# Four hidden tiles of the `down` projection by half products, in pieces between the `up` tiles

## The chip, the core and the metric

The kernel runs on one core of a Trainium2 chip. The metric is device time in microseconds (us), from the start of one execution to its end. A core has TensorE (PE; its weight loads are listed as PEld), VectorE (DVE), ScalarE (ACT), GpSimd (POOL), which here mostly issues DMAs, and SyncE (SP), which issues the other DMAs. TensorE writes into PSUM, whose tiles are allocated as banks of 128 partitions by 512 float32 values; VectorE and ScalarE read results from there. Each engine works through its own list of instructions in order and waits by semaphores for the others.

## The reference

One decoder layer on 512 positions of width 1024: a mixer (pooling and sparse attention), then a gated MLP with a short convolution. The change is in the MLP:

```python
h = rms_norm(x, ffn_norm_g[l])
gate_pre, val = jnp.split(h @ w_up[l], 2, axis=-1)      # D_FF = 2816
gate_c = causal_dwconv(gate_pre, conv_w[l], conv_b[l])  # width 3
x = x + (jax.nn.silu(gate_c) * val) @ w_down[l]
```

The hidden width of 2816 is 22 tiles of 128, called `f` below; the output width of 1024 is 8 tiles.

## The kernel before

**Precision.** Every float32 operand `v` is split into a part `hi` (type fp32r) and the rest `lo = v - hi`; a product is the sum of three matmuls: hi by hi, hi by lo, lo by hi. `split` (line 462) does it with one ScalarE copy and one VectorE subtraction. `split_by_dma` (line 1269) does it with two ScalarE passes and an accumulating DMA issued by POOL, and without VectorE.

**The order.** The code does not issue instructions where it names them. `Plan` (line 117) notes each one with its reads and writes, prices it (`price`), tries several orders in a model of the engines and DMA queues (`run`, `dues`, `emit`) and in the end writes out the best order, engine by engine interleaved in time (lines 429 to 431; for this reason all instructions have line 431 in the profile). In the MLP TensorE's own order is that of the code; the other engines are ordered by the time at which TensorE needs their results. In PSUM the planner tracks a whole tile at a time, unless its name is in the set `fine`, in which case it tracks columns (line 190); nothing in this kernel adds a name to it. Semaphores between engines are made afterwards, from the order that was written out.

**Memory.** Most data lies in 60 pages of 128 x 512 values (`page`). A page named by `soon` is for weights prepared ahead; these are given out in the order of the code and only while more than `AHEAD` = 4 pages are free. Weights land in rings of three buffers, `wraw`, `whi`, `wlo`, 1024 values wide (`ring`).

**Half products.** A product of a 2 x 2 block matrix of weights with a 2 x 2 block matrix of data (two groups of tiles by two halves of 256 positions) is done with seven block products instead of eight. It needs sums of weight blocks, made by VectorE (`half_weights`, line 1410), and sums of the data (`y_sums`, line 1338). `product` (line 1147) issues one block product: for each tile three matmuls of 256 columns. The partial sums stay in three banks `bx`, `by`, `bq`; where a second result continues from a first, ScalarE copies `bx` into `by` and TensorE goes on adding there.

**The loop.** For `f` from 0 to 21 (line 1487) the kernel computes the gate and value tiles (`up_plain` for tile 0, `up_fast`, line 1441, for the others, by seven half products of four tiles each), the convolution and SiLU (`conv`), and splits the result `y` (`split_y`, line 1349). The last two products of a tile, `end1` and `end2`, are held back (`held`) and issued inside the next tile.

**`down` before.** The 22 hidden tiles are taken in groups: `GROUPS` has tiles 0 to 4, 5 to 9 and 10 to 13, and tiles 14 to 21 (from `LAST`) are left for the end. `dn_group` (line 1398) makes, for one group, eight pieces, one for each output tile: load 128 x (640 or 512) weights, split them, 15 or 12 matmuls of 512 columns into bank `sc`, and add the result to `x2[f]` on VectorE. The pieces go into the list `fills`. At `f` = 6, 12 and 16 (`AT`) a group is put into the list, and the four numbers of `FILL[f]` say how many pieces are taken out before the tile and at three places within `up_fast`: `n1` after the first `bq` product or the held product in its place, `n3` after the first `by` product and the second held one, `n2` after the second `bx` product. What is left goes behind the last tile. Then `dz_fast` (line 1508) does tiles 14 to 21 by half products, four pairs of output tiles, and stores the results.

Of the kernel before, what the change touches and what calls it, by code (L numbers as in the profile page):

```python
# [9 lines left out]
F32R = mybir.dt.float32r  # L10
I32 = mybir.dt.int32
AF = mybir.ActivationFunctionType
# [3 lines left out]
P = 128  # L16
T = 512
# [6 lines left out]
FF = 2816  # L24
KF = 22
LAST = 14
GROUPS = ((0, 5), (5, 10), (10, 14))
EPS = 1e-6
BIG = 1e30

# [24 lines left out]
PLAIN = (0,)  # L55
DIRECT = (0,)
FASTM = (0, 1)
AT = (6, 12, 16)
FILL = {f: (0, 0, 0, 0) for f in range(22)}
FILL.update({f: (0, 1, 1, 0) for f in (7, 10, 13, 16,)})  # L60
FILL.update({f: (0, 1, 0, 0) for f in (6, 8, 9, 11, 12, 14, 15, 17, 18, 19,)})
TRIES = 12
RESERVE = 3
CUTS = (1, 2)
# [4 lines left out]
SHARE = 1.5  # L69
LANDS = (0.8, 0.8, 1.2, 1.2, 2.0, 2.0)  # L70
TRIALS = ((0.5, RATE), (0.8, RATE), (1.4, RATE), (0.8, 0.9 * RATE))
AHEAD = 4
RUN = 12


# [357 lines left out]

@with_exitstack
def hybrid_layer(ctx: ExitStack, tc: tile.TileContext, xT, xa, pos, par, cst, poolw, w1, wa, wb, wf,
                 wpo, wno, wout, wup, wdn, wdz, out):
    nc = tc.nc
    pl = Plan(nc)
    PE, ACT, DVE, POOL, SP = pl.engines
# [8 lines left out]
    def page(name, shape=(P, T), dt=F32):  # L448
        return pl.tile(sb, shape, dt, name, "pg", PAGES)
# [12 lines left out]
    def split(dst_hi, dst_lo, src, scale=None):  # L462
        if scale is None:
            ACT.activation(dst_hi, src, AF.Copy)
            DVE.tensor_sub(dst_lo, src, f32(dst_hi))
        else:
            ACT.activation(dst_hi, src, AF.Copy, scale=scale)
            DVE.scalar_tensor_tensor(dst_lo, src, scale, f32(dst_hi), op0=ALU.mult, op1=ALU.subtract)
# [40 lines left out]
    H2 = T // 2  # L509
# [18 lines left out]
    w2 = R("w2").rearrange("p (a b) -> p a b", a=2)  # L528
# [109 lines left out]
    A, KQ, KH, KL = (ang[:, i] for i in range(4))  # L638
# [47 lines left out]
    for c, (k0, k1) in enumerate(((0, 3), (3, 6), (6, 8))):  # L686
        raw = ring("wraw")
        SP.dma_start(raw[:, :(k1 - k0) * 280], flat(wb[:, k0:k1]))
        for j in range(k1 - k0):
            home = ("pp", 10) if len(bw) < 5 else ("pt", 6)  # L690
            hi, lo = (pl.tile(sb, (P, 280), F32R, n, home[0], home[1]) for n in ("bh", "bl"))
# [42 lines left out]
    for t in range(NT):  # L734
        x, y = qp[t], kp[t]
# [182 lines left out]
    x = keep("kcx", (64, 1, DH))  # L918
# [248 lines left out]
    for c in range(4):  # L1167
        if c not in FASTM:
# [3 lines left out]
            for a in range(2):  # L1172
                f, o = 2 * c + a, a * 512
# [19 lines left out]
        rg, hi, lo = ring("wraw"), ring("whi", F32R), ring("wlo", F32R)  # L1193
        SP.dma_start(rg, flat(wno[c]))
        split(hi[:, :T], lo[:, :T], rg[:, :T])
        a11, a12, a21, a22 = (rg[:, q * H2:(q + 1) * H2] for q in range(4))
        s3, e3, hi2, lo2 = soon("s3")[:, :H2], soon("sh", F32R), soon("sh", F32R), soon("sl", F32R)
# [7 lines left out]
        w11, w12, w2, w4 = ((hi[:, q * H2:(q + 1) * H2], lo[:, q * H2:(q + 1) * H2]) for q in range(4))  # L1205
        w1, w5 = ((hi2[:, q], lo2[:, q]) for q in (L, Rr))
        w3 = e3[:, L], e3[:, Rr]
        bx, bq, by = any_bank(), any_bank(), any_bank()
# [6 lines left out]
        half = page("u1")  # L1215
# [117 lines left out]
        ACT.activation(t, t, AF.Silu)  # L1333
        return t

    yth, ytl, ylast = {}, {}, {}

    def y_sums(k):
        b1, b2 = ylast[k], ylast[k + 4]
        ta, tb = page("ta"), page("tb")  # L1340
        DVE.tensor_sub(ta[:, :H2], b1[:, :H2], b1[:, H2:])
        DVE.tensor_sub(tb[:, :H2], b2[:, H2:], b1[:, H2:])
        DVE.scalar_tensor_tensor(ta[:, H2:], ta[:, :H2], -1.0, b2[:, H2:], op0=ALU.mult, op1=ALU.subtract)
        DVE.scalar_tensor_tensor(tb[:, H2:], ta[:, H2:], -1.0, b2[:, :H2], op0=ALU.mult, op1=ALU.subtract)
        for i, x in ((0, ta), (1, tb)):
            yth[k - LAST, i], ytl[k - LAST, i] = page("yth", dt=F32R), page("ytl", dt=F32R)
            split(yth[k - LAST, i], ytl[k - LAST, i], x)

    def split_y(f, y):
        yh[f], yl[f] = page("yh", dt=F32R), page("yl", dt=F32R)  # L1350
        split(yh[f], yl[f], y)
        if f >= LAST:
            ylast[f] = y
        if f > LAST + 3:
            y_sums(f - 4)

    def up_plain(f):
        pts = []
# [28 lines left out]
    held, fills = [], []  # L1387
# [10 lines left out]
    def dn_group(g):  # L1398
        lo, hi = GROUPS[g]

        def one(f, free):
            wh, wl = weights(wdn[f, :, lo * P:hi * P], (hi - lo) * P, "v")
            pt = any_bank() if free else bank("sc", (P, 2, T))[:, 0]
            mm3(pt, wh, wl, yh, yl, lo, hi, koff=lo, nk=hi, first=lo)
            DVE.tensor_add(x2[f], pt, x2[f])

        for f in range(KD):
            fills.append(lambda free, f=f: one(f, free))

    def half_weights(first, second, w, dma, gate):  # L1410
        rg, r1, r2 = ring("wraw"), soon("r1"), soon("r2")
# [74 lines left out]

    for f in range(KF):
        if f in AT:
            dn_group(AT.index(f))
        fill(FILL[f][0], True)  # L1490
        if f in PLAIN:
            up_plain(f)
        else:
            up_fast(f, *FILL[f][1:])
# [42 lines left out]
    pl.emit(TRIES, RESERVE)  # L1537


_INS = ["xT", "xa", "pos", "par", "cst", "poolw", "w1", "wa", "wb", "wf", "wpo", "wno", "wout", "wup", "wdn", "wdz"]  # L1540


def _layout(x, positions, mix_norm_g, w_in, q_norm_g, k_norm_g, cmp_pe, cmp_w1, cmp_w2, pool_w,
            pool_scale, w_pool_out, w_nsa_out, w_out, ffn_norm_g, w_up, conv_w, conv_b, w_down):
    import numpy as np

    f = lambda a: np.asarray(a)
    x, w_in = f(x)[0], f(w_in)[0]
    A = {}
    A["xT"] = x.T.reshape(KD, P, T)  # L1550
    p = f(positions)[0]
    cpos = np.zeros(P, p.dtype)
    idx = np.minimum(16 * np.arange(32) + 31, T - 1)
    cpos[:32] = p[idx]
    cpos[32:64] = p[idx]
    A["pos"] = np.concatenate([p.reshape(NT, P).T, cpos[:, None]], axis=1)

    def cols(a, n):
        return f(a)[0].reshape(n, P).T

    def stack2(a):
        return a.reshape(16, 2, DH, -1).transpose(1, 2, 0, 3).reshape(P, 16, -1)

    pe = np.stack([stack2(f(cmp_pe)[0, i][..., None])[..., 0] for i in range(2)], axis=1)
    A["w1"] = np.stack([stack2(f(cmp_w1)[0, i]) for i in range(2)])
    ngv = np.concatenate([f(q_norm_g)[0], f(k_norm_g)[0].reshape(-1)])
    par = {
        "mixg": cols(mix_norm_g, KD), "ffng": cols(ffn_norm_g, KD), "pscale": cols(pool_scale, 4),
        "convw": f(conv_w)[0].reshape(3, KF, P).transpose(2, 1, 0).reshape(P, -1),
        "convb": cols(conv_b, KF), "pe": pe.reshape(P, -1),  # L1570
        "w2": f(cmp_w2)[0].transpose(1, 0, 2).reshape(P, -1),
        "ng": np.broadcast_to(ngv, (P, 256)),
    }
    A["par"] = np.concatenate([par[n] for n in PAR], axis=1)
    A["xa"] = np.concatenate([A["par"][:, :16], A["xT"][0]], axis=1)
    q, kk = np.arange(P)[:, None], np.arange(P)[None, :]
    mask = np.zeros((P, NT, P), np.float32)
    mask[:, 3] = np.where(kk <= q, 0.0, BIG)
    t = np.arange(T).reshape(NT, P).T
    n = np.arange(32)  # L1580
    cmask = np.where((16 * n + 31 <= t[:, :, None]) & (n < NB), 0.0, BIG)
    recip = np.zeros((NT, 16), np.float32)
    for i in range(NT):
        recip[i] = np.float32(1) / np.minimum(np.arange(16) + 1, 2 << i).astype(np.float32)
    cst = {
        "ident": np.eye(P), "mask": mask.reshape(P, -1), "cmask": cmask.reshape(P, -1),
        "valid": (t >= 31).astype(np.float32), "recip": np.broadcast_to(recip.reshape(-1), (P, 64)),
        "inv": np.broadcast_to(np.array(INV, np.float32), (P, 8)),
    }
    A["cst"] = np.concatenate([cst[n_].astype(np.float32) for n_ in CST], axis=1)  # L1590
    A["poolw"] = f(pool_w)[0].transpose(1, 0, 2)
    kv = w_in[:, 1024:1792].reshape(D, 6, 128)
    wi = w_in.reshape(KD, P, -1)
    kvk = kv.reshape(KD, P, 6, 128)
    A["wa"] = np.concatenate([wi[:, :, 512:1024], kvk[:, :, 2], kvk[:, :, 4]], axis=2)
    wb = np.concatenate([kvk[:, :, 3], kvk[:, :, 5], wi[:, :, 1792:1816]], axis=2)
    A["wb"] = wb.transpose(1, 0, 2)

    def tiles(w):
        k, m = w.shape  # L1600
        return w.reshape(k // P, P, m // P, P).transpose(2, 1, 0, 3)

    A["wf"] = np.concatenate([tiles(kv[:, 0]), tiles(kv[:, 1]), tiles(w_in[:, :512]),
                              tiles(w_in[:, 1816:])])
    A["wpo"] = tiles(f(w_pool_out)[0]).reshape(4, 2, P, 4, P).transpose(0, 2, 1, 3, 4)
    A["wno"] = tiles(f(w_nsa_out)[0]).reshape(4, 2, P, 2, 2, P).transpose(0, 2, 1, 4, 3, 5).reshape(4, P, 8, P)
    A["wout"] = tiles(f(w_out)[0])
    A["wup"] = tiles(f(w_up)[0]).reshape(2, KF, P, KD, P).transpose(1, 0, 2, 3, 4)
    wd = tiles(f(w_down)[0])
    A["wdn"] = wd[:, :, :LAST].reshape(KD, P, LAST * P)  # L1610
    A["wdz"] = wd[:, :, LAST:]
    return {n_: np.ascontiguousarray(A[n_]) for n_ in _INS}

# [18 lines left out]
```

## Time and profile before

| | |
|---|---|
| Median of 3 runs | 680.2 us (679.52 to 680.35) |
| The profiled execution | 680.19 us |
| Its span, first to last instruction | 678.1 us |
| Tiles 1 to 21 of `up` start | 349.75 to 605.73 us |
| The eight first pieces of `down` run from | 399.38 us |
| Last five pieces, then the final results | from 621.4, from 635.0 us |

The profile is of one execution. Busy times of VectorE and ScalarE are durations of instructions, which can overlap a little when they follow each other directly. A chain of waits follows the work that ended last back through what released it. A window gives the busy time of each engine in a stretch of time. Group rows give count, busy time, the mean duration of one, then the idle time of the engine just before them and what ended it. `L431` is the planner's line and says nothing of the source; groups are told apart by tile names: `gp`, `gh` and `th` are data of `up`, `sc` is the bank of the `down` pieces, `yh`, `yl`, `yth`, `ytl` are data of `down`, `x` and `o` residual and output.

### The profile page before, as it was taken

Reading aid. Unit: us, or ns where it says so; the run is one execution under the profiler, and the core shown is the slowest. Engines: PE = TensorE matmul, PEld = TensorE weight load, DVE = VectorE, ACT = ScalarE, POOL = GpSimd, SP = SyncE. Lnnn points to the kernel's source line nnn. Section 1 sums busy time; section 2 is a strip of 40 time slices with the busy share of each in tenths; the row PEclk is TensorE's granted clock in tenths of the full one; section 3 lists DMA queues with packets and bytes.
Section 4 is the critical chain, followed back from the end, with each engine's and each line's share of the span. In section 5 each row is a group of like instructions: output and inputs, shape, how many; then the busy total and the mean of one; then the engine's idle time right before and its main releaser. Section 6 shows DMA issues by size and latency. Waiting matters only on the chain.

```text
span 678.1 us, 11960 instructions
## 1 busy us (share of the span) xinstructions
PE 673.4 (99%) x4294; PEld 609.1 (90%) x4294; DVE 545.2 (80%) x1198; ACT 458.7 (68%) x857; POOL 109.0 (16%) x138
## 2 busy tenths in 40 slices
PE   9999999999999999999999999999999999999998
PEld 8898888888888888988889999999999999999997
DVE  6869678788887867788888998887778787899983
ACT  7666577776677765347788867677657677675741
POOL 0010111010110110001322312222213122220121
PEclk9999999999999999999999999999999999999999
DMA  8469646263565555846977958779858678553774
GB/s 306 145 156 264 172 108 187 67 171 99 143 167 134 143 134 181 312 146 203 232 166 176 194 144 203 194 170 208 190 160 190 168 161 211 134 115 129 191 181 109
DMA packets 51179, 116.41 MB, mean 172 GB/s; under 512 B 5808, under 2 KB 9264, under 8 KB 51120
## 3 DMA queue, kind: packets, MB, share of 16 engines
q1 hardware_dynamic: 32688, 76.44, 33.9%
q0 software_dynamic: 18288, 39.07, 32.6%
q8 instruction: 34, 0.56, 0.3%
q14 instruction: 25, 0.20, 0.1%
q10 hardware_dynamic: 144, 0.14, 0.1%
HBM read 70.28 MB, written 6.29 MB: 113 GB/s over the span
## 4 chain that ended last, share of the span: by engine, by line
PE 99%; DMA 1%; SPq 0%; ACT 0%; DVE 0%; issue 0%
PE mm L431 38%; PE tr L431 36%; PE sc L431 13%; PE av L431 12%; DMA wraw<-wa 1%; SPq L431 0%; ACT whi L431 0%; DVE o L431 0%
## 5 line engine op out<-in xcount | busy, mean ns | idle before, releaser
L431 ACT ACTIVATE whi<-wraw 128x1024 fp32r<-128x1024 f32 (+4 forms) x99 | 91.9, 930 | 40.9 <-PE sc L431 14.7
L431 DVE TENSOR_TENSOR wlo<-wraw,whi 128x1024 fp32r<-128x1024 f32 (+3 forms) x73 | 74.0, 1015 | 5.1 <-ACT whi L431 4.3
L431 PE MATMUL tr<-tl,sh 128*128 128x256 f32 x261 | 73.1, 280 | 0.0
L431 PE MATMUL mm<-xh,whi 128*128 128x512 f32 x176 | 70.7, 402 | 0.0
L431 PE MATMUL tr<-th,sh 128*128 128x256 f32 x250 | 70.4, 282 | 0.0
L431 PE MATMUL tr<-th,sl 128*128 128x256 f32 x250 | 70.4, 282 | 0.0
L431 PE MATMUL mm<-xh,wlo 128*128 128x512 f32 x176 | 68.9, 391 | 0.0
L431 PE MATMUL mm<-xl,whi 128*128 128x512 f32 x176 | 68.6, 390 | 0.0
L431 POOL DMA_DIRECT2D sl<-r x46 | 39.8, 866 | 149.8 <-ACT sl L431 104.8
L431 POOL DMA_DIRECT2D wlo<-wraw x26 | 22.3, 858 | 231.7 <-ACT wlo L431 178.8
L431 PEld LDWEIGHTS tr<-tl,sh 128*128 128x128 f32 x261 | 49.3, 189 | 0.2
L431 PEld LDWEIGHTS tr<-th,sh 128*128 128x128 f32 x250 | 47.0, 188 | 0.7
L431 PEld LDWEIGHTS tr<-th,sl 128*128 128x128 f32 x250 | 47.0, 188 | 0.0
L431 ACT ACTIVATE wlo<-wraw 128x1024 fp32r<-128x1024 f32 x26 | 27.6, 1060 | 19.3 <-PE mm L431 18.4
L431 PEld LDWEIGHTS mm<-xh,wlo 128*128 128x128 f32 x176 | 33.0, 188 | 7.3
L431 PEld LDWEIGHTS mm<-xl,whi 128*128 128x128 f32 x176 | 33.1, 188 | 6.2
L431 ACT ACTIVATE pp<-pp,asm 128x384 f32<-128x384 f32 (+3 forms) x64 | 35.4, 556 | 4.9 <-DVE asm L431 4.9
L431 PEld LDWEIGHTS mm<-xh,whi 128*128 128x128 f32 x176 | 33.1, 188 | 6.1
L431 DVE SCALAR_TENSOR_TENSOR ft<-fg,pr,ft 128x511 f32<-128x511 f32 (+1 forms) x44 | 32.9, 749 | 7.0 <-ACT ft L431 6.3
L431 POOL DMA_DIRECT2D sl<-wraw x26 | 22.4, 862 | 84.7 <-ACT sl L431 68.5
L431 ACT ACTIVATE sh<-wraw 128x512 fp32r<-128x512 f32 x52 | 32.3, 620 | 4.1 <-DVE wraw L431 4.0
L431 ACT ACTIVATE sl<-r 128x512 fp32r<-128x512 f32 x46 | 28.6, 622 | 9.3 <-DMA r<-wup 5.4
(443 smaller groups left out, 2134.4 us busy)
## 6 DMA issues: line engine op xcount, KB each, us to landing
wlo<-wraw POOLq DMA_DIRECT2D x26, 512.0 KB, 4.6
wraw<-wup SPq DMA_DIRECT2D x23, 512.0 KB, 4.1
sl<-r POOLq DMA_DIRECT2D x46, 256.0 KB, 4.8
wraw<-wf SPq DMA_DIRECT2D x22, 512.0 KB, 3.6
r<-wup SPq DMA_DIRECT2D x42, 256.0 KB, 5.7
sl<-wraw POOLq DMA_DIRECT2D x26, 256.0 KB, 4.2
wraw<-wdn SPq DMA_DIRECT2D x16, 320.0 KB, 3.7
sl<-s POOLq DMA_DIRECT2D x17, 256.0 KB, 5.0
```

Source lines behind the costliest of these rows:

```text
L431: getattr(self.real[o.eng], method)(*a, **kw)
```

## The change

Group 1 becomes tiles 5 to 8 and is done by half products (`hp_group`) for four pairs of output tiles; group 2 becomes tiles 9 to 13, as ordinary pieces. Each pair is four pieces of two, two, two and one products; the sums over `y` are made when tiles 7 and 8 are split. All four pairs run in tiles 11 to 15. The three partial sums of a pair lie in one tile of two rows of 512: `bx` and `bq` in one row, `by` in the other, and the tile is put into `fine`. `AHEAD` goes from 4 to 2. The weights come in an array of their own, `wdh`.

```diff
@@ -24,7 +24,8 @@
 FF = 2816
 KF = 22
 LAST = 14
-GROUPS = ((0, 5), (5, 10), (10, 14))
+GROUPS = ((0, 5), (5, 9), (9, 14))
+HALVED = 1
 EPS = 1e-6
 BIG = 1e30
 
@@ -55,10 +56,12 @@
 PLAIN = (0,)
 DIRECT = (0,)
 FASTM = (0, 1)
-AT = (6, 12, 16)
+AT = (6, 11, 16)
 FILL = {f: (0, 0, 0, 0) for f in range(22)}
-FILL.update({f: (0, 1, 1, 0) for f in (7, 10, 13, 16,)})
-FILL.update({f: (0, 1, 0, 0) for f in (6, 8, 9, 11, 12, 14, 15, 17, 18, 19,)})
+FILL.update({f: (0, 1, 1, 0) for f in (7, 9, 10)})
+FILL.update({f: (0, 1, 0, 0) for f in (6, 8, 16, 17, 18)})
+FILL.update({f: (0, 1, 1, 1) for f in (11, 12, 13, 14)})
+FILL.update({15: (1, 1, 1, 1)})
 TRIES = 12
 RESERVE = 3
 CUTS = (1, 2)
@@ -69,7 +72,7 @@
 SHARE = 1.5
 LANDS = (0.8, 0.8, 1.2, 1.2, 2.0, 2.0)
 TRIALS = ((0.5, RATE), (0.8, RATE), (1.4, RATE), (0.8, 0.9 * RATE))
-AHEAD = 4
+AHEAD = 2
 RUN = 12
 
 
...
@@ -1333,26 +1336,29 @@
         ACT.activation(t, t, AF.Silu)
         return t
 
-    yth, ytl, ylast = {}, {}, {}
-
-    def y_sums(k):
-        b1, b2 = ylast[k], ylast[k + 4]
+    yth, ytl, ylast, ysh, ysl = {}, {}, {}, {}, {}
+
+    def y_sums(k, e, hi, lo, k0):
+        b1, b2 = ylast[k], ylast[e]
         ta, tb = page("ta"), page("tb")
         DVE.tensor_sub(ta[:, :H2], b1[:, :H2], b1[:, H2:])
         DVE.tensor_sub(tb[:, :H2], b2[:, H2:], b1[:, H2:])
         DVE.scalar_tensor_tensor(ta[:, H2:], ta[:, :H2], -1.0, b2[:, H2:], op0=ALU.mult, op1=ALU.subtract)
         DVE.scalar_tensor_tensor(tb[:, H2:], ta[:, H2:], -1.0, b2[:, :H2], op0=ALU.mult, op1=ALU.subtract)
         for i, x in ((0, ta), (1, tb)):
-            yth[k - LAST, i], ytl[k - LAST, i] = page("yth", dt=F32R), page("ytl", dt=F32R)
-            split(yth[k - LAST, i], ytl[k - LAST, i], x)
+            hi[k - k0, i], lo[k - k0, i] = page("yth", dt=F32R), page("ytl", dt=F32R)
+            split(hi[k - k0, i], lo[k - k0, i], x)
 
     def split_y(f, y):
         yh[f], yl[f] = page("yh", dt=F32R), page("yl", dt=F32R)
         split(yh[f], yl[f], y)
-        if f >= LAST:
+        h0, h1 = GROUPS[HALVED]
+        if f >= LAST or h0 <= f < h1:
             ylast[f] = y
+        if h0 + 1 < f < h1:
+            y_sums(f - 2, f, ysh, ysl, h0)
         if f > LAST + 3:
-            y_sums(f - 4)
+            y_sums(f - 4, f, yth, ytl, LAST)
 
     def up_plain(f):
         pts = []
@@ -1406,6 +1412,67 @@
 
         for f in range(KD):
             fills.append(lambda free, f=f: one(f, free))
+
+    def hp_group(g):
+        lo = GROUPS[g][0]
+        Le, Ri = slice(0, H2), slice(H2, T)
+
+        def mv(i, half):
+            c = slice(half * H2, (half + 1) * H2)
+            if i < 2:
+                return tuple((lambda k, q=q: q[lo + 2 * i + k][:, c]) for q in (yh, yl))
+            return tuple((lambda k, q=q: q[k, i - 2][:, c]) for q in (ysh, ysl))
+
+        def pair(c):
+            f, e, w = 2 * c, 2 * c + 1, []
+            b = []
+
+            def one():
+                rg, hi, lw = ring("wraw"), ring("whi", F32R), ring("wlo", F32R)
+                SP.dma_start(rg, flat(wdh[c]))
+                split(hi[:, :T], lw[:, :T], rg[:, :T])
+                a11, a12, a21, a22 = (rg[:, q * H2:(q + 1) * H2] for q in range(4))
+                s3, e3, hi2, lo2 = soon("s3")[:, :H2], soon("sh", F32R), soon("sh", F32R), soon("sl", F32R)
+                DVE.tensor_add(s3, a11, a21)
+                DVE.tensor_add(a21, a21, a22)
+                DVE.tensor_add(a11, a11, a21)
+                DVE.tensor_add(a12, a12, a11)
+                split_by_dma(hi2, lo2, rg[:, T:])
+                split(hi[:, T:], lw[:, T:], rg[:, :T])
+                split(e3[:, Le], e3[:, Ri], s3)
+                w11, w12, w2, w4 = ((hi[:, q * H2:(q + 1) * H2], lw[:, q * H2:(q + 1) * H2]) for q in range(4))
+                w.extend((w11, w12, (hi2[:, Le], lo2[:, Le]), w2, (e3[:, Le], e3[:, Ri]), w4, (hi2[:, Ri], lo2[:, Ri])))
+                t = bank("sc", (P, 2, T))
+                pl.fine.add(t.tensor.name)
+                bx, bq, by = t[:, 0, :H2], t[:, 0, H2:], t[:, 1, :H2]
+                b.extend((bx, bq, by))
+                product(bx, w[0], mv(0, 0), True, 2)
+                ACT.activation(by, bx, AF.Copy)
+                product(bq, w[2], mv(2, 0), False, 2)
+                DVE.tensor_sub(x2[e][:, Ri], x2[e][:, Ri], bq)
+
+            def two():
+                bx, bq, by = b
+                product(by, w[3], mv(2, 1), False, 2)
+                DVE.tensor_add(x2[f][:, Ri], x2[f][:, Ri], by)
+                product(bx, w[1], mv(1, 0), False, 2)
+                DVE.tensor_add(x2[f][:, Le], x2[f][:, Le], bx)
+
+            def three():
+                bx, bq, by = b
+                product(by, w[4], mv(3, 0), False, 2)
+                DVE.tensor_sub(x2[e][:, Ri], x2[e][:, Ri], by)
+                product(bq, w[5], mv(1, 1), False, 2)
+                DVE.tensor_add(x2[f][:, Ri], x2[f][:, Ri], bq)
+
+            def four():
+                product(b[2], w[6], mv(3, 1), False, 2)
+                DVE.tensor_sub(x2[e][:, Le], x2[e][:, Le], b[2])
+
+            fills.extend((lambda free, q=q: q()) for q in (one, two, three, four))
+
+        for c in range(4):
+            pair(c)
 
     def half_weights(first, second, w, dma, gate):
         rg, r1, r2 = ring("wraw"), soon("r1"), soon("r2")
@@ -1486,7 +1553,8 @@
 
     for f in range(KF):
         if f in AT:
-            dn_group(AT.index(f))
+            g = AT.index(f)
+            (hp_group if g == HALVED else dn_group)(g)
         fill(FILL[f][0], True)
         if f in PLAIN:
             up_plain(f)
...
@@ -1608,6 +1676,8 @@
     A["wup"] = tiles(f(w_up)[0]).reshape(2, KF, P, KD, P).transpose(1, 0, 2, 3, 4)
     wd = tiles(f(w_down)[0])
     A["wdn"] = wd[:, :, :LAST].reshape(KD, P, LAST * P)
+    h0, h1 = GROUPS[HALVED]
+    A["wdh"] = wd[:, :, h0:h1].reshape(4, 2, P, h1 - h0, P).transpose(0, 2, 1, 3, 4).reshape(4, P, 2 * (h1 - h0), P)
     A["wdz"] = wd[:, :, LAST:]
     return {n_: np.ascontiguousarray(A[n_]) for n_ in _INS}
```

More of the change, by code (lines that the diff above doesn't have):

```diff
@@ L435, in hybrid_layer @@
 def hybrid_layer(ctx: ExitStack, tc: tile.TileContext, xT, xa, pos, par, cst, poolw, w1, wa, wb, wf,
-                 wpo, wno, wout, wup, wdn, wdz, out):
+                 wpo, wno, wout, wup, wdn, wdh, wdz, out):
     nc = tc.nc
@@ L1537, in hybrid_layer @@
     pl.emit(TRIES, RESERVE)
-_INS = ["xT", "xa", "pos", "par", "cst", "poolw", "w1", "wa", "wb", "wf", "wpo", "wno", "wout", "wup", "wdn", "wdz"]
+_INS = ["xT", "xa", "pos", "par", "cst", "poolw", "w1", "wa", "wb", "wf", "wpo", "wno", "wout", "wup", "wdn", "wdh", "wdz"]
 def _layout(x, positions, mix_norm_g, w_in, q_norm_g, k_norm_g, cmp_pe, cmp_w1, cmp_w2, pool_w,
```

## The prediction

> **What bounds the kernel now.** I read the page's first part, then its chain, then the waits of TensorE alone, then windows cut at the starts of the `up` tiles.
>
> ```profile
> span 678.1 us, 11960 instructions
> PE 673.4 (99%) x4294; PEld 609.1 (90%) x4294; DVE 545.2 (80%) x1198; ACT 458.7 (68%) x857; POOL 109.0 (16%) x138
> PE 99%; DMA 1%; SPq 0%; ACT 0%; DVE 0%; issue 0%
> PE mm L431 <- POOL ones L431: 1.0, 1, 1.0
> PE sc L431 <- ACT whi L431: 0.3, 1, 0.3
> ```
>
> TensorE is the bound without rest: it carries 99% of the chain, and its list of waits holds two entries, 1.3 us together, both in the first microseconds. So time can be saved only by taking columns away from TensorE, and any new wait of TensorE adds its full length. There is no slack on its side to absorb one.
>
> The windows of the stage that changes (columns: window, its length, busy time of PE, PEld, DVE, ACT, POOL with counts, clock, DMA share, GB/s); tile 1 starts at 349.75, tile 6 at 396.55, tile 11 at 470.15, tile 16 at 540.33, the final results at 635:
>
> ```profile
> 349.75:396.55 46.80, 46.80 (x398) 46.80 (x396) 42.13 (x72) 38.84 (x72) 11.20 (x13) 1.00 0.84 189
> 396.55:409.91 13.36, 13.36 (x102) 12.74 (x100) 12.46 (x23) 8.96 (x18) 3.44 (x4) 1.00 0.47 102
> 396.55:470.15 73.60, 73.60 (x527) 69.34 (x526) 63.55 (x109) 52.54 (x94) 18.08 (x21) 1.00 0.74 173
> 470.15:540.33 70.18, 70.18 (x513) 66.53 (x511) 53.79 (x91) 46.67 (x83) 15.52 (x18) 1.00 0.77 185
> 540.33:637.00 96.67, 96.67 (x690) 91.03 (x689) 83.31 (x149) 67.72 (x120) 19.86 (x23) 1.00 0.65 155
> ```
>
> PE fills every window at clock 1.00. VectorE is second: 90% in tiles 1 to 5, 12.46 of 13.36 (93%) in tile 6, 77% in tiles 11 to 15. It is the engine to watch.
>
> **The change part by part: TensorE.** Three rows of the chain give the price of a matmul.
>
> ```profile
> 399.55 3.43 PE sc L431 x15
> 615.82 2.74 PE mm L431 x12
> 588.87 2.84 PE tr L431 x24
> ```
>
> A `down` piece of five tiles is 15 matmuls of 512 columns, 3.43 us; one of four is 12, 2.74 us (0.228 each). Twenty-four of 256 columns take 2.84 us (0.1183 each; the duration of 0.28 in the timeline overlaps the next). Groups of 5, 5, 4 become 5, halved 4, 5: so eight pieces of 12 wide matmuls go, 8 x 2.74 = 21.9 us. Four pairs come, each of seven products of two tiles by three matmuls, 4 x 42 = 168 narrow matmuls, which is seven times the row of 24: 7 x 2.84 = 19.9 us. **TensorE gets 2.0 us less.** Every other matmul stays, in other places.
>
> **VectorE and ScalarE.** What is removed and added, by the groups with shapes apart:
>
> ```profile
> L431 DVE TENSOR_TENSOR wlo<-wraw,whi 128x512 fp32r<-128x512 f32 x12 | 8.2, 684 | 0.1
> L431 DVE TENSOR_TENSOR x<-sc,x 128x512 f32<-128x512 f32 x18 | 12.4, 690 | 14.3 <-PE sc L431 14.2
> L431 DVE TENSOR_TENSOR fg<-fg,rb 128x256 f32<-128x256 f32 x21 | 8.8, 421 | 0.4
> L431 ACT ACTIVATE whi<-wraw 128x512 fp32r<-128x512 f32 x12 | 7.6, 631 | 7.2 <-PE mm L431 3.6 <-DVE wraw L431 1.7 <-PE sc L431 1.1
> L431 ACT ACTIVATE sh<-wraw 128x512 fp32r<-128x512 f32 x52 | 32.3, 620 | 4.1 <-DVE wraw L431 4.0
> L431 ACT ACTIVATE tr<-mm 128x256 f32<-128x256 f32 x25 | 9.2, 369 | 11.5 <-PE mm L431 11.2
> ```
>
> VectorE loses eight splits and eight additions, 8 x (0.684 + 0.690) = 11.0 us. A pair brings two splits of 512, four weight sums and one split of 256, and seven additions of 256: 2 x 0.684 + 12 x 0.421 = 6.4 us, four pairs 25.7. The sums of `y` for the two tile pairs (four of 256, two splits of 512) bring 2 x 3.1 = 6.1. Net 20.8 us by durations. But durations overlap:
>
> ```profile
> 587.10 0.68 DVE L431 SCALAR_TENSOR_TENSOR y<-y,ft 128x512 f32<-128x512 f32 x1
> 587.70 0.68 DVE L431 TENSOR_TENSOR sl<-wraw,sh 128x512 fp32r<-128x512 f32 x1
> 588.30 0.42 DVE L431 TENSOR_TENSOR ta<-y 128x256 f32<-128x256 f32 x1
> 588.64 0.68 DVE L431 TENSOR_TENSOR yl<-y,yh 128x512 fp32r<-128x512 f32 x1
> ```
>
> From start to start it is 0.60 us for 512 and 0.34 for 256, so the net is 4 x 5.3 + 5.1 - 9.6 = 16.7 us. From tile 6 to the final results VectorE had 63.55 + 53.79 + 83.31 = 200.65 us busy in 240.4; it will have 217 to 221 in 238.4, 91 to 93%. Inside tiles 11 to 15, where all four pairs lie, it is tighter: 53.79 less six five-tile pieces (some 1.4 each, from these starts) leaves about 45; with 21 to 26 that makes 66 to 71 in 69.6 us (five tiles of seven products, 5 x 9.94, and 19.9), 95 to 102%. That is above anything the trace shows. I still cost it at nothing: the two-piece tile 10 ahead and tiles 16 to 18 behind (some 85%) have room, and the second halves of `conv` and the splits of `y` for tiles 14 and 15 are needed only at the end. The price if this cover fails is the second rival.
>
> ScalarE: per pair four passes of 512 (two of 0.631, two of 0.620) and two of 256 (0.369), 3.2 us, four times 13.0, plus 2.5 for the sums, less 8 x 0.631: net 10.4 us. In tiles 11 to 15 that makes (46.7 - 4.4 + 13.0) / 69.6 = 79%: covered by TensorE.
>
> **Queues.** SP issues four loads of 512 KB for eight of 256; POOL gets four accumulating DMAs.
>
> ```profile
> wraw<-wdn SPq DMA_DIRECT2D x8, 256.0 KB, 2.9
> wraw<-wup SPq DMA_DIRECT2D x23, 512.0 KB, 4.1
> sl<-wraw POOLq DMA_DIRECT2D x26, 256.0 KB, 4.2
> SPq L431 <- DMA sl<-wraw: 86.4, 19, 10.3
> ```
>
> SP already waits 86.4 us for such accumulations to give a slot of `wraw` back, with the next `up` tile's load behind it, and TensorE never feels it. Each pair's slot is held until its accumulation lands, 4.2 us longer than a plain slot. Four more such waits lie in about 70 us; I take nothing, bounds 0 and 1 us.
>
> **New waits.** The additions into `x2` wait for TensorE seven times a pair, where eight pieces waited once each; today VectorE idles about 14.2 / 15 = 0.95 us for each such wait, with the next tile's evacuations behind it. In the other direction TensorE waits for readers of PSUM. Between two pieces lie at least two `up` products, 2.8 us, so `by` is read in time (0.2 + 0.42 + 0.05, below). One place is closer: in `one` the products `bx` and `bq` follow each other directly, and both lie in one 512-column row of the same tile, while ScalarE copies `bx`. Does a product wait for a reader of other columns in its row? This trace has no product and reader in that position; the nearest rows are two readers, ScalarE's and then VectorE's:
>
> ```profile
> 60.57 1.20 ACT L431 ACTIVATE kt<-tr 64x512 fp32r<-64x512 f32 x2
> 62.53 0.59 ACT L431 ACTIVATE kt<-tr 64x512 fp32r<-64x512 f32 x1 [0.76 <-DVE kt L431]
> 61.80 0.69 DVE L431 TENSOR_TENSOR kt<-tr,kt 64x512 fp32r<-64x512 f32 x1 [0.89 <-ACT kt L431]
> ```
>
> The two take turns, without overlap, though the code (lines 764 to 769) copies `pt` into `y` without needing VectorE's result. So a wait for the whole row is likely, in the order in which the planner wrote the instructions. The planner does not see it: the new line puts the tile into `fine`, so it tracks columns. The price of one wait:
>
> ```profile
> 5.98 0.42 ACT whi L431
> 6.45 0.74 PE sc L431 x4
> 674.48 0.28 PE L431 MATMUL tr<-yth,sl 128*128 128x256 f32 x1
> 674.80 0.42 DVE o L431
> ```
>
> A reader starts 0.32 us after the last matmul's start, which is 0.20 after the next could start; the copy takes 0.37; TensorE restarts 0.05 after its reader's end: 0.62 us. It falls due only if the copy was written between the two tiles of `bq` (0.36 us apart): later, it follows `bq` and costs TensorE nothing. With ScalarE busy four fifths of the time I put that at one in three. Bounds for the four pairs: 0 and 2.5 us; I take 0.2, near the lower, since none or one is the usual count.
>
> [...]
>
> **Sum:** -2.0 (TensorE) + 0.2 (waits) + 0 (VectorE, queues) = -1.8 us against the profiled execution, 680.19 us (span 678.1 and 2.1 around it). The median of the runs, 680.2, is the same. Forecast **678.4 us**.
>
> **The rivals.** *Shared rows give it back.* `bx` and `bq` share a row, and three VectorE reads of that row per pair can also fall between the tiles of a product (0.42 instead of 0.37, 0.67 each). Two to four such waits cost 1.2 to 2.7 us: 679.4 to 680.9, say 679.9. For it: the alternating readers, the planner's blindness. Against it: pieces 2.8 us apart, so most reads are over before.
>
> [...]
>
> *VectorE becomes the bound in tiles 11 to 15.* If its 66 to 71 us cannot leave the stretch, and it holds 93% at most (the fullest tile above), the stretch lasts 71 to 76.5 us, 1.5 to 7 more than TensorE needs. I take 5, with its extra idle waits for products: 680.19 - 2.0 + 5 = 683.2, slower. It decides as soon as VectorE is over 3.4 us late for what TensorE needs next (1.4 us beyond the gain). For it: 95 to 102%. Against it: tiles 1 to 5, at 90% and with no `down` piece to rest in, show no wait of TensorE.
>
> *The new order loses elsewhere.* The planner lays out everything anew, with two free pages kept instead of four. In tile 15 thirty of the 60 pages hold split results and sums (22 before), and 42 at the end (40). A late weight load there, or at the first final product, costs 1 to 5 us: 679.2 to 683.2, say 681.7.
>
> **How the numbers follow.** A measurement here can tell about 0.2% (1.4 us) from no change: faster is below 678.8, slower above 681.6. Forecast (0 or 1 wait, 678.0 to 678.8): 0.48, faster but for 0.03. Shared rows: 0.28, of which 0.03 faster, 0.23 same, 0.02 slower. VectorE as bound: 0.14, of which 0.02 same, 0.12 slower. Elsewhere: 0.10, of which 0.04 same, 0.06 slower. Together faster 0.48, same 0.32, slower 0.20. The range goes from 677.8, the whole saving with some tenths more, to 682.0, which takes in the shared rows and the near parts of the last two rivals; about 0.15 lies beyond.
>
> **What would show it.** Right: 168 more narrow and 96 fewer wide matmuls, PE busy down by 2 us, its list of waits still with no entry over a few tenths after 345 us, VectorE 91 to 95% from tile 6 on. Shared rows: entries of PE waiting for ACT `sc` or DVE `x`, of about 0.6 each, between tiles 11 and 16. VectorE: PE waits for DVE results of the weights or of `y` in the same stretch, growing towards tile 15. The sum itself is wrong if 24 narrow matmuls of the new pieces take other than 2.84 us, and the forecast is wrong if TensorE's waits in the whole span exceed about 2 us.

## The result, and the profile after

| | before | after |
|---|---|---|
| Median | 680.08 us (679.52 to 680.35, 6 runs) | 683.93 us (682.82 to 685.6, 6 runs) |
| Profiled execution | 680.19 us | 683.77 us |
| Its span | 678.1 us | 682.0 us |

The change makes the kernel slower: the ratio of after to before is 1.0059 [1.0045, 1.0072], about 3.9 us. That is past the upper end of the predicted range.

Summary and engine totals of the page of after:

```profile
span 682.0 us, 12193 instructions
PE 673.3 (99%) x4366; PEld 611.4 (90%) x4366; DVE 560.1 (82%) x1246; ACT 466.8 (68%) x877; POOL 112.6 (17%) x142
```

The total of TensorE, 673.3 us against 673.4, hides the saving. A matmul's record of 0.28 us outlasts the 0.118 us to the next start, so a wait shows as idle time only in part; and a matmul that starts after a wait is recorded with 0.39 us. The list of its waits says more (engine, tile, line, what it waited for: us in total, times, longest):

```profile
PE sc L434 <- DVE x L434: 2.6, 5, 0.5
PE tr L434 <- ACT u L434: 1.2, 2, 0.8
PE mm L434 <- POOL ones L434: 1.0, 1, 1.0
PE sc L434 <- DMA sl<-wraw: 0.3, 1, 0.3
```

Before, nothing stood in this list after 345 us. Now there are five waits of `sc`, the tile that holds `bx`, `bq` and `by`, for VectorE results `x`; two waits for ScalarE's `u` (a third is too short for the list); and one for an accumulating DMA. Here is the first of the five in the timeline of after (start, length, engine, line, operation, output<-inputs, and in brackets the idle time before it and what ended it; lines of PE, then one of DVE):

```profile
485.31 0.28 PE L434 MATMUL sc<-yth,sh 128*128 128x256 f32 x1
485.43 0.28 PE L434 MATMUL sc<-yh,whi 128*128 128x256 f32 x1
485.55 0.28 PE L434 MATMUL sc<-yl,whi 128*128 128x256 f32 x1
485.67 0.28 PE L434 MATMUL sc<-yh,wlo 128*128 128x256 f32 x1
486.46 0.39 PE L434 MATMUL sc<-yh,whi 128*128 128x256 f32 x1 [0.51 <-DVE x L434]
486.68 0.28 PE L434 MATMUL sc<-yl,whi 128*128 128x256 f32 x1
...
485.99 0.42 DVE L434 TENSOR_TENSOR x<-x,sc 128x256 f32<-128x256 f32 x1 [0.64 <-PE sc L434]
```

This is piece `three`. The product into `by` ends with the matmul at 485.31. Then comes the product into `bq`: three matmuls for its first tile (485.43 to 485.67) and three for its second. VectorE's subtraction from `by` could have started at 485.63, 0.32 us after the last matmul of `by`, but it starts at 485.99, 0.32 after the third matmul of `bq`. So it waited for the first tile of `bq` as well. The second tile of `bq` starts at 486.46, 0.05 us after the read ends at 486.41, so it waited for a read of `by`. Both waits are between **different rows of the shared tile**: `by` lies in one row of 512, `bq` in the other. TensorE could have gone on at 485.79; it loses 0.67 us there, and 0.11 more because the next matmul starts 0.22 later instead of 0.118. That makes 0.78 us. The other four waits look alike (519.07 to 519.86, 524.10 to 524.89, 535.52 to 536.31, 540.55 to 541.35), always between the two tiles of the second product of a piece (`bq` in `three`, `bx` in `two`), and always released by the read of `by` from the first product. Together: 3.9 us.

The other losses, from the timeline of TensorE. At the first `bq` of tile 11 it waits 0.6 us (476.46 to 477.06) for the accumulation that makes `lo2`. In tiles 19, 20 and 21 it waits about 1.1, 0.3 and 0.6 us (2.0 with the slower restarts) for data of `up` from ScalarE. ScalarE's own lines in tiles 18 and 19 of after show why:

```profile
584.66 0.63 ACT L434 ACTIVATE sh<-wraw 128x512 fp32r<-128x512 f32 x1 [1.39 <-DMA sl<-s]
587.17 0.82 ACT L434 ACTIVATE ft<-fg,pr 128x512 f32<-128x512 f32 x1 [1.88 <-DMA sl<-r]
587.89 1.04 ACT L434 ACTIVATE whi<-wraw 128x1024 fp32r<-128x1024 f32 x1
588.84 0.36 ACT L434 ACTIVATE u<-tr 128x256 f32<-128x256 f32 x1
```

ScalarE stands still for 1.39 and 1.88 us until accumulating DMAs land, and `u`, for which TensorE waits, stands behind them.

The balance of the two profiled executions: matmuls -2.0; five waits +3.9; first `bq` +0.6; tiles 19 to 21 +2.0; tile 1 starts earlier, at 349.00 instead of 349.75, -0.7. The sum is +3.8; the spans differ by 3.9. The last of these terms isn't shown to be a gain of the change: in the kernel e1 below, whose lists are the same as those of after, tile 1 starts at 349.65.

### The profile page after: what moved, and what is told of

It is laid out like the page before. It is cut to its first block, busy times and chain, and to the rows that moved or that the text cites. A ratio compares the mean times of both kernels' runs of the same rounds, so it can differ in the third digit from the quotient of the medians.

```text
span 682.0 us, 12193 instructions
## 1 busy us (share of the span) xinstructions
PE 673.3 (99%) x4366; PEld 611.4 (90%) x4366; DVE 560.1 (82%) x1246; ACT 466.8 (68%) x877; POOL 112.6 (17%) x142
## 4 chain that ended last, share of the span: by engine, by line
PE 90%; issue 3%; DMA 3%; DVE 2%; POOL 1%; ACT 1%; SPq 0%; POOLq 0%; ACTq 0%; DVEq 0%
PE mm L434 38%; PE tr L434 32%; PE av L434 11%; PE sc L434 10%; DMA sl<-r 1%; DMA sl<-wraw 1%; DMA r<-wup 1%; POOL sl L434 1%; DVE wraw L434 0%; ACT whi L434 0%; DVE x L434 0%; DVE wlo L434 0%; DVE ft L434 0%; SPq L434 0%; DVE y L434 0%
## 5 line engine op out<-in xcount | busy, mean ns | idle before, releaser
L434 POOL DMA_DIRECT2D sl<-wraw x30 | 25.9, 864 | 95.9 <-ACT sl L434 74.2
L434 ACT ACTIVATE sh<-wraw 128x512 fp32r<-128x512 f32 x56 | 34.8, 621 | 5.2 <-DVE wraw L434 3.5
L434 ACT ACTIVATE sh<-r 128x512 fp32r<-128x512 f32 x50 | 31.0, 620 | 4.1 <-DVE r L434 2.6
```

The source lines that it names most:

```text
L434: getattr(self.real[o.eng], method)(*a, **kw)
```

## The experiments

Theory A says that the five waits come from the order that was written out. Semaphores are made from that order, and they treat the two-row tile as one thing. The planner, told by `fine` to track columns, sees no conflict and may put a read of `by` between the two tiles of the next product. In its written order of after this is so five times, each time on VectorE, at the five places of the trace. Theory B, its rival, is the one of the prediction: VectorE is too full in tiles 11 to 15, so that the reads come late, and the loss is a lack of VectorE time that another order would only move.

**Second tile directly behind the first (e1_glue).** Only the interleaving of the engines changes: in a half product the second tile's matmuls are written out right behind the first's. Each engine's own list stays that of after, instruction by instruction.

```diff
+    def glued(self, order):
+        told, out = set(), []
+        for o in order:
+            while o is not None and o.i not in told and o.deps <= told:
+                out.append(o)
+                told.add(o.i)
+                o = o.glue
+        return out
...
-        for o in best[1]:
+        for o in self.glued(best[1]):
...
+            if k and bank_.tensor.name in pl.fine:
+                pl.ops[-2].glue = pl.last()
```

> The changed kernel with one thing different: where a half product writes into the tile shared by bx, bq and by, its second tile of matmuls is written out directly behind the first, so that no reader of the shared tile stands between them. Each engine's own list of instructions stays the same, row by row; only who waits for whom differs. Theory A (the five waits of TensorE for VectorE, 0.78 us each, come from a reader of by standing between the two tiles of bq, though it lies in another row): all five go, 683.9 - 3.9 = 680.0 us, the waits in tiles 19 to 21 (2.0 us) and at the first bq (0.6 us) stay. Rival B (VectorE is overloaded in tiles 11 to 15 and TensorE only meets it there): the waits move to other products of the same stretch, 683 to 684 us.

Measured: 680.71 us (678.84 to 683.62, 12 runs), ratio to before 1.0011 [1.0001, 1.0021]. TensorE's waits in the profile of this kernel:

```profile
PE tr L444 <- ACT u L444: 2.6, 3, 1.9
...
PE sc L444 <- ACT whi L444: 0.5, 1, 0.5
```

All five waits for VectorE are gone. At the same place of the same lists the timeline now reads:

```profile
489.42 0.28 PE L444 MATMUL sc<-yh,whi 128*128 128x256 f32 x1
...
489.65 0.28 PE L444 MATMUL sc<-yh,wlo 128*128 128x256 f32 x1
489.77 0.28 PE L444 MATMUL sc<-yh,whi 128*128 128x256 f32 x1
...
490.01 0.28 PE L444 MATMUL sc<-yh,wlo 128*128 128x256 f32 x1
490.12 0.28 PE L444 MATMUL tr<-th,sh 128*128 128x256 f32 x1
...
490.32 0.42 DVE L444 TENSOR_TENSOR x<-x,sc 128x256 f32<-128x256 f32 x1 [0.99 <-PE sc L444]
```

The six matmuls of `bq` follow each other, `up` goes on, and the same read of `by` starts 0.31 us after the last of them without holding anyone. VectorE was not the limit. The windows of 470 to 541 us of before, after and this kernel, in that order (window, its length, busy time of PE, PEld, DVE, ACT, POOL with counts, clock, DMA share, GB/s):

```profile
470.00:541.00 71.00, 71.00 (x519) 67.35 (x518) 54.61 (x92) 47.20 (x84) 15.52 (x18) 1.00 0.76 183
```

```profile
470.00:541.00 71.00, 68.47 (x562) 66.97 (x560) 61.19 (x121) 51.96 (x97) 19.33 (x23) 1.00 0.77 176
```

```profile
470.00:541.00 71.00, 71.00 (x585) 70.04 (x585) 62.80 (x125) 54.08 (x101) 19.46 (x23) 1.00 0.79 177
```

VectorE is busy for 61.19 us (86%) in after. Without the waits it is busier, 62.80 (88%), and TensorE is full. (This kernel's profile runs some 4 us later here, so its window doesn't hold quite the same work.) Theory B needed the waits to move to other products of this stretch, and there are none in it. The median fell by 3.2 us, less than the 3.9 of the waits. Of the waits that were expected to stay, the one at the first `bq` is gone in this profile, and tiles 19 to 21 lose 1.6 us. The profiled run, the slowest of the twelve, shows why that one was slow: a wait in tile 6 with something new behind it (the last section).

That wait is a difference between two runs, for the program is that of after up to the first new piece, and after's profile has no wait there. In both, the load of tile 6's weights is issued as soon as an accumulation out of `wraw` has landed; in after this is 4.8 us before the tile, and the load takes 3.9 us; in e1 it is 3.8 us before, and the load takes 5.3. In before it was 7.8. So the new order leaves less room at this place, and the landings of the run decide what it costs. The runs of the new kernels also lie further apart than those of before: 678.84 to 683.62 here, 679.22 to 680.62 for before beside it.

**Another order, waits counted beforehand (e7_ahead1), and the same one glued (e8_ahead1_glue).** The first is after with one free page kept instead of two, so that the planner writes another order. In it four readers stand between the two tiles of a product: two copies by ScalarE and two reads by VectorE. The second adds the edit of e1; the lists of all engines are the same.

```diff
-AHEAD = 2
+AHEAD = 1
```

> The changed kernel with AHEAD = 1 instead of 2, which gives another order. In the order that this one writes out, four readers of the shared tile stand between the two tiles of a product: two copies of bx by ScalarE inside bq, and two VectorE readers. Theory A: exactly four waits of about 0.75 us there, two of them for ACT, at those places and nowhere else in the new pieces, 3.0 us in all. Rival B (VectorE is overloaded): waits for DVE grow towards tile 15, with no relation to the written order.

> As e7_ahead1, with the second tile of a product written out directly behind the first; every engine's list is that of e7_ahead1. Theory A: 3.0 us faster than e7_ahead1, no wait left in the new pieces; 678 to 681 us with whatever waits for late loads this order has. Rival B: as e7_ahead1.

Measured: 682.97 us (682.87 to 683.71, 5 runs), ratio 1.0045 [1.0033, 1.0057], and glued 680.4 us (679.98 to 683.45, 11 runs), ratio 1.0011 [1.0002, 1.0021]. TensorE's waits, first without and then with the edit:

```profile
PE tr L434 <- ACT u L434: 1.6, 2, 1.0
PE sc L434 <- DVE x L434: 1.0, 2, 0.5
...
PE sc L434 <- ACT sc L434: 0.9, 2, 0.5
```

```profile
PE tr L444 <- ACT u L444: 1.0, 1, 1.0
...
PE tr L444 <- ACT tr L444: 0.5, 1, 0.5
```

Two of each kind, as counted, 0.73 to 0.78 us each; with the edit none of the four. One more wait in this stretch, 0.9 us for `u` at 518.09, is not of this kind and is also absent with the edit. The difference of the medians, 2.6 us, fits the four waits (3.0) about as well as the first pair did.

**The planner tracks the whole tile (e9_nofine_fill19).** The line that put the tile into `fine` is taken out, so planner and semaphores agree; `FILL` has one more place, tile 19, as in e5 below.

```diff
-                pl.fine.add(t.tensor.name)
```

> The changed kernel without the line that puts the shared tile into fine, so that the planner itself keeps TensorE from a product in the shared tile until all readers are done; one ordinary piece in tile 19, as in e5_glue_fill19 (without that the planner finds no order). Theory A, with the waits now planned: 12 places (copy of bx before bq, by read before bx, by read before bq, four pairs), each 0.62 to 0.78 us, 7.4 to 9.4 us over the 679.7 of e5_glue_fill19: 687 to 689 us. If semaphores did not cover the whole tile: about 680 us.

Measured: 688.08 us (687.68 to 688.58, 4 runs), ratio 1.0117 [1.0104, 1.0131]: the slowest kernel of all. Its list of TensorE's waits begins:

```profile
PE sc L434 <- DVE x L434: 4.4, 8, 0.6
PE sc L434 <- ACT sc L434: 2.6, 4, 1.3
```

Twelve waits: four pairs, in each the copy of `bx` and two reads of `by`. That is every reader which is followed by another product of its piece. So a planner that knows the whole tile doesn't avoid these waits by itself: it puts the readers ahead of the next product, which then waits for them. With `fine`, seven of the twelve readers happened to be written behind that product, where they cost nothing.

**One more place for a piece (e5_glue_fill19).** This asks whether the waits of tiles 19 to 21 belong to the spot in which the order ran short. It is e1 with a piece of `down` also in tile 19.

```diff
-FILL.update({f: (0, 1, 0, 0) for f in (6, 8, 16, 17, 18)})
+FILL.update({f: (0, 1, 0, 0) for f in (6, 8, 16, 17, 18, 19)})
```

> As e1_glue, and one of the five ordinary pieces that are left for the end runs in tile 19, as in the kernel before; TensorE's work is the same. Theory C (three bare tiles in a row, 19 to 21, leave the weights of the next tile no time to land): the 2.0 us of waits for ACT u go too, 678.0 to 678.5 us. Rival D (the pages are short whatever the order): the waits stay or move, 680.0 us.

Measured: 679.74 us (678.74 to 684.48, 11 runs), ratio 1.0004 [0.9989, 1.0019]. TensorE's waits:

```profile
PE tr L444 <- ACT u L444: 1.5, 1, 1.5
...
PE sc L444 <- ACT whi L444: 0.8, 1, 0.8
PE sc L444 <- DMA sl<-wraw: 0.3, 1, 0.3
```

The waits of tiles 19 to 21 are gone, and the median is 4.2 us below that of after. But 1.8 us are now lost in tile 6 (398.00 to 399.80), before the first new piece, and 0.5 at the first `bq` again. In tile 6 ScalarE stands behind the load of the tile's weights, and `u` behind their split:

```profile
397.90 1.06 ACT L444 ACTIVATE whi<-wraw 128x1024 fp32r<-128x1024 f32 x1 [2.92 <-DMA wraw<-wup]
```

The gain of 2.0 us on TensorE is given back in this way.

**Later landings in the planner's model (e10_glue_fill19_lands, and once more as e13_lands_again).** If the rest comes from DMAs that land later than the planner thinks, larger delays in its model should help.

```diff
-LANDS = (0.8, 0.8, 1.2, 1.2, 2.0, 2.0)
-TRIALS = ((0.5, RATE), (0.8, RATE), (1.4, RATE), (0.8, 0.9 * RATE))
+LANDS = (0.8, 1.2, 1.6, 2.0, 2.4, 2.8)
+TRIALS = ((0.8, RATE), (1.4, RATE), (2.2, RATE), (1.4, 0.9 * RATE))
```

> As e5_glue_fill19, with the planner told that transfers land later (LANDS up to 2.8 instead of 2.0 us, trials up to 2.2). If what is left after the shared tile is late landings ahead of ScalarE (tile 6 and the first bq of tile 11): fewer of these waits, 678.2 to 679 us and faster than the kernel before. If the lateness is not of that kind: 679.7 us as e5_glue_fill19.

> e10_glue_fill19_lands once more beside the others, for its ratio on another chip: 679.6 us, ratio 0.9993; the waits left in its profile fall on other tiles than before if they come from landings that vary from run to run, on the same tiles if the order alone makes them.

Measured: 679.58 us (677.86 to 682.26, 12 runs), ratio 0.9993 [0.9983, 1.0002], and on another chip 680.14 us (679.16 to 681.7, 11 runs), ratio 1.0001 [0.9992, 1.0010]. Waits of the first and of the second:

```profile
PE tr L444 <- ACT u L444: 1.5, 1, 1.5
PE tr L444 <- DMA sl<-r: 0.9, 1, 0.9
```

```profile
PE tr L444 <- ACT u L444: 1.5, 1, 1.5
PE tr L444 <- DMA sl<-r: 1.0, 1, 1.0
```

Both profiles wait at the same two places, near 382 us and near 608.6 us, so these are the places that this order leaves exposed. It does not follow that every run loses as much there: e10's runs go from 677.86 to 682.26 us, and both profiled ones lie above their median. The fastest reach the time that was forecast. The second wait in e10, on ScalarE:

```profile
606.70 0.63 ACT L444 ACTIVATE sh<-s 128x512 fp32r<-128x512 f32 x1 [3.31 <-DMA sl<-r]
...
610.02 0.36 ACT L444 ACTIVATE u<-tr 128x256 f32<-128x256 f32 x1
```

Again ScalarE stands behind an accumulating DMA, 3.31 us, and `u` is late. This version, the best of the study, can't be told from before by its median.

**No accumulating DMA for the new weights (e11_fill19_nodma, and with e10's delays e12_fill19_nodma_lands).** If the four new accumulations cause the rest, splitting `hi2`, `lo2` on VectorE should give it back.

```diff
-                split_by_dma(hi2, lo2, rg[:, T:])
...
+                split(hi2, lo2, rg[:, T:])
```

> As e5_glue_fill19, but each pair's last weight sums are split by VectorE (one subtraction of 512 more a pair) and not by an accumulating DMA. If what is left after the shared tile is late landings, and the four accumulations with their long hold on a wraw slot have a part in it: the wait at the first bq goes, fewer waits of TensorE for ACT u, 678.2 to 679.2 us. If VectorE is near its limit after all (rival B): 2.4 us more of its time in tiles 11 to 15 shows as waits for DVE, 680 to 682 us. If neither: 679.7 us.

> As e11_fill19_nodma with the planner told of later landings as in e10_glue_fill19_lands: the try for a kernel faster than both. If late landings are what is left: 678.0 to 679.0 us, ratio to the kernel before below 0.999. If the order cannot help: 679.6 us as e10_glue_fill19_lands.

Measured: 681.64 us (679.88 to 686.3, 12 runs), ratio 1.0035 [1.0019, 1.0052], and 680.79 us (680.39 to 682.88, 11 runs), ratio 1.0016 [1.0007, 1.0024]. The wait at the first `bq` went, and one for VectorE came instead. TensorE's waits in the first of the two kernels (the second also has one for `x` and one for `u`, of about 1.0 and 0.9 us):

```profile
PE tr L444 <- ACT tr L444: 1.5, 1, 1.5
...
PE sc L444 <- DVE x L444: 0.5, 1, 0.5
PE mm L444 <- ACT sl L444: 0.3, 1, 0.3
```

In e11 the entry for `x` is the known wait at a place that the edit of e1 doesn't close: the read of `by` was written between the two products of a piece, not between the tiles of one. VectorE had been idle for 0.47 us before it, so it wasn't late (in e12 it was, by 0.2 us):

```profile
537.48 0.42 DVE L444 TENSOR_TENSOR x<-x,sc 128x256 f32<-128x256 f32 x1 [0.47 <-PE sc L444]
```

The median of e11 lies where the rival with the full VectorE was expected (680 to 682 us), but its sign, waits for VectorE in tiles 11 to 15, is this one wait of 0.8 us. The largest loss, 1.8 us, comes at 599.88, where ScalarE stands behind an accumulation for `up`; about 1.5 us more go near 612 and from 645 us on. So without the new accumulations the wait at the first `bq` goes, and the other losses move to new places and do not shrink. As the planner lays out the whole kernel anew, the runs don't show what part the four had in the rest.

**`AHEAD` alone (e3_before_ahead2).** The kernel before with two free pages kept instead of four.

```diff
-AHEAD = 4
+AHEAD = 2
```

> The kernel before with AHEAD = 2 instead of 4 and nothing else. If keeping only two free pages is by itself what makes ScalarE late in tiles 19 to 21: 681 to 682 us, with waits of TensorE for ACT u late in the up tiles. If it needs the new pieces and their pages: 680.1 us, no wait.

Measured: 680.52 us (680.08 to 680.94, 11 runs), ratio 1.0009 [1.0000, 1.0017], with one new wait:

```profile
PE tr L431 <- ACT u L431: 0.2, 1, 0.2
```

It lies at tile 21 and costs 0.5 us with its restart. So the smaller reserve of pages alone brings a wait of the kind seen in tiles 19 to 21, but a quarter of its size.

## Why the prediction was wrong

- **TensorE, -2.0 us: right.** 72 more matmuls (4366 for 4294) are the forecast 168 narrow ones less 96 wide ones. Tile 13 of after, from start to start, is 9.93 + 30 x 0.118 = 13.47 us long, which is the forecast work and nothing else (tile 12 is as long). Its window:

```profile
501.81:515.28 13.47, 13.47 (x116) 13.47 (x115) 12.44 (x25) 10.58 (x20) 3.81 (x5) 1.00 0.80 163
```

- **New waits, taken as 0.2 us with bounds 0 and 2.5: the step that failed.** The five waits made 3.9 us. Its mechanism was half right: a product does wait for a reader of other columns, if the reader was written between its two tiles. Three things were wrong. First, the cover is the whole tile and not the row of 512. The sentence "`by` is read in time", argued from 2.8 us between two pieces, looked at the next use of `by` and not at the other row, whose product follows `by` at once within the same piece. That sentence ruled out the very reads that became the five waits, while the copy of `bx`, which it saw as the close place, was never between two tiles in after (twice in e7). Second, the count: 12 places, not the 4 of this term, and 5 of them hit. Third, the price: 0.67 was right for the wait, but TensorE also restarts slowly (0.22 us to the next start instead of 0.118), which makes 0.78.
- **"Shared rows give it back"** had the right kind of mechanism, readers between the two tiles of a product, at 2 to 4 waits and 679.9 us, but counted readers of the same row, and the five came from the other. 5 waits at 0.78 and the losses elsewhere carried the time past it. The planner's blindness, which spoke for it, is just what decided; "most reads are over before", which spoke against it, was the failed step once more.
- **"VectorE becomes the bound": wrong, though its time, 683.2, is near the measured one.** Its total rose by 14.9 us (545.2 to 560.1), near the 16.7 that the prediction got by starts (a pair has six additions into `x2` and not seven, which makes 15.3); but of this only 6.6 us lie in 470 to 541 us (8.2 in e1), and it was at 86% there, not 95 to 102%. The prediction had put all of the pairs' added work inside the stretch. e1 shows directly that the same lists run through without a wait for VectorE, so that the time came near is luck.
- **Queues, taken as nothing (bounds 0 and 1 us):** the 0.6 us at the first `bq` is inside the bounds. It was one TensorE wait for a new accumulation. But "TensorE never feels it", read from the profile of before, does not hold for the new order: in e1 and e5 the load that waits for an accumulation came late for tile 6, and TensorE lost 2.2 and 1.8 us.
- **"The new order loses elsewhere", 1 to 5 us at a chance of 0.10: it happened.** 2.0 us went in tiles 19 to 21, by ScalarE waiting for landings, not in tile 15. The rows of ScalarE ended by a DMA show the kind of wait; the forecast had cost ScalarE by its busy time only (79%, covered). The sum had this at nothing, and so it is the second term that was mis-sized.

**What stays open.** Without the five waits the kernel is level with before in its median, not 2 us faster. In their profiles the new orders lost 2 to 5 us at other places. ScalarE stood behind an accumulating DMA (608.6 us in e10; 599.9 us in e11) or behind a load that had itself waited for one (tile 6), and near 382 us TensorE waited for an accumulation itself. That these DMAs are the cause is read from the profiles; no run shows the kernel without those that `up` needs. Whether the 60 pages force that wasn't settled: the one-page and the two-page reserve differ little (680.4 and 680.71 glued), and the reserve of three or four pages wasn't tried with the change, for the planner finds no order in 60 pages then. `by` in a tile of its own wasn't tried either: earlier stages use both rows of `sc` as one tile, and with the six other tiles the kernel has allocated eight banks; whether one more fits was not shown.

## What to carry to other kernels

Where one tile holds several partial sums, ask what the semaphores cover and not what a planner tracks, and count the readers that stand between two matmuls of one product in the order that is written out: here each cost 0.73 to 0.78 us, and the same reads behind the product cost nothing. When an engine is at 99%, a saving of 2 us is worth as much as the new order's worst three waits, so price the engines that feed it by what they stand behind (accumulating DMAs here, and loads that wait for them), and not by their busy share. An engine that ends a wait need not be the one that is short: keep its list and move only the order between the engines, and see whether the wait stays.

## What was not expected of the hardware

**A wait of 2 us cost 3.7.** In the profiled run of e1 TensorE waits in tile 6 for ScalarE, which has the split of the next weights ahead of `u`. The windows around it (columns as above; the eighth figure is the granted clock):

```profile
399.00:400.00 1.00, 0.08 (x1) 0.08 (x1) 0.37 (x1) 0.87 (x3) 0.00 (x0) 1.00 0.50 192
400.00:401.00 1.00, 1.00 (x6) 1.00 (x7) 1.00 (x3) 0.64 (x2) 0.00 (x0) 0.64 0.06 23
401.00:402.00 1.00, 1.00 (x7) 1.00 (x7) 1.00 (x2) 1.00 (x3) 0.00 (x0) 0.50 0.00 0
402.00:403.00 1.00, 1.00 (x5) 0.90 (x5) 1.00 (x4) 0.85 (x2) 0.86 (x1) 0.50 0.00 0
403.00:404.00 1.00, 1.00 (x5) 0.76 (x4) 1.00 (x3) 0.00 (x0) 0.00 (x0) 0.66 0.54 94
404.00:405.00 1.00, 1.00 (x6) 0.84 (x5) 1.00 (x2) 0.00 (x0) 0.00 (x0) 1.00 0.98 168
```

And its timeline:

```profile
397.74 0.28 PE L444 MATMUL mm<-gp,wlo 128*128 128x256 f32 x1
399.92 0.39 PE L444 MATMUL tr<-th,sh 128*128 128x256 f32 x1 [1.90 <-ACT u L444]
...
400.88 0.41 PE L444 MATMUL tr<-th,sl 128*128 128x256 f32 x1
401.10 0.41 PE L444 MATMUL tr<-th,sh 128*128 128x256 f32 x1
```

The wait is 2.06 us long. Soon after it the granted clock is 0.50, by the shares of these windows from about 400.3 to 403.7 us, and narrow matmuls start 0.21 us apart instead of 0.118: some 1.6 us more. Waits of 1.68 us (e5) and 1.66 us (e11) in the profiles left the clock at 1.00. Between 1.68 and 2.06 us nothing was measured, and no run shows what lowers the clock. Mean clocks of 0.995 to 0.997 (0.997 in this run) also stand with some of the slowest timed runs (684.48 in e5; 684.14, 684.37, 685.14 and 686.3 in e11), which have no trace, so that a wait of this kind behind them is likely but not shown.

**Each wait in the pieces cost TensorE a second start.** After each of the five waits of after the next matmul starts 0.22 or 0.23 us later instead of 0.118 (486.46 to 486.68 in the first), so 0.67 becomes 0.78.
